# Choosing experts and building their gate rows side by side in one stage: broadcast one-hots, the factor on ScalarE, staging by 32 tokens

## The chip, the cores and the metric

One core of one Trainium2 chip runs the whole program. The metric is the device time of one execution in microseconds (us). TensorE, VectorE, ScalarE, GpSimd and SyncE each work off their own queue in order. In the profile's rows they are PE (with PEld for its weight loads), DVE, ACT, POOL and SP.

## The reference

Two transformer blocks over 512 tokens of width 1024, in fp32. The part that matters is the expert layer (`peer`) at the end of the first block:

```python
def chunk_fn(hc):
    q = (hc @ w_query).reshape(PEER_CHUNK, PEER_HEADS, PEER_KEY_DIM)
    s1 = jnp.einsum('chk,nk->chn', q[..., :PEER_HALF_DIM], keys_1)
    s2 = jnp.einsum('chk,nk->chn', q[..., PEER_HALF_DIM:], keys_2)
    v1, i1 = lax.top_k(s1, PEER_TOPK_HALF)
    v2, i2 = lax.top_k(s2, PEER_TOPK_HALF)
    cand = (v1[..., :, None] + v2[..., None, :]).reshape(PEER_CHUNK, PEER_HEADS, -1)
    cand_idx = (i1[..., :, None] * N_KEYS + i2[..., None, :]).reshape(PEER_CHUNK, PEER_HEADS, -1)
    top_s, pos = lax.top_k(cand, PEER_TOPK)
    experts = jnp.take_along_axis(cand_idx, pos, axis=-1)
    gate = jax.nn.softmax(top_s.astype(jnp.float32), axis=-1).astype(hc.dtype)
    u = jnp.take(expert_u, experts, axis=0)
    act = jax.nn.gelu(jnp.einsum('chkd,cd->chk', u, hc))
    v = jnp.take(expert_v, experts, axis=0)
    return jnp.einsum('chk,chkd->cd', gate * act, v)
```

There are 8 heads, 16 chosen experts per head (128 per token) and 16384 experts, addressed by two indices of 128 values each.

## The kernel before

Three of the four token tiles (384 tokens) are computed densely: the activations of all 16384 experts, in 128 groups of 128 experts, are made by TensorE, multiplied by a gate matrix that is zero where an expert was not chosen, and multiplied with the V matrix. The fourth tile gathers its own experts' rows by indirect DMA (`pick`) and reduces them on VectorE.

Work goes by an order written out by hand (`manual_schedule`): each engine takes its instructions in program order. The unit of that order is a *slot*, made by `slot()`. Slot i issues the load of expert group i+3 (`u_load`, SP queue), prepares group i+2 (`u_prep`: ScalarE makes `uhi`, VectorE makes `ulo`), runs what is passed as `dve`, then multiplies group i (`u_main`: 24 matrix products into `act`, below called a U block), runs what is passed as `after`, applies the gelu (`ga`, ScalarE), writes it to DRAM (`asc`, issued by ScalarE), issues some of the waiting gate pieces (`piece`, SP) and some gathered rows (`pick`, a GpSimd gather and one VectorE operation on `row`). There are three `uhi` and three `ulo` buffers and two `act` buffers in PSUM.

Before the change two loops of slots follow each other:

- **Choosing.** For each of the four token tiles, the generator `choose(t)` is stepped once per slot. A tile has seven steps of VectorE work: candidates and the first and second half of the top 16 (steps 1, 2), the `ge` comparison and its products (3), reductions and products that read the two indices out (4 to 6), softmax (7, with an `Exp` on ScalarE). The seventh step falls into the slot of the next tile's first, so there are 24 slots, and one more (`CGAP`).
- **Gates.** The gate matrix of 8 tokens is a *unit*, and there are 48. `gate_rows` makes for each token a one-hot row `ob` over the second index and a one-hot row `oa` over the first, times the gate, each [128 chosen, 128]. `gate_mm` multiplies them one slot later on TensorE (8 products into `pg`), and ScalarE copies `pg` into the staging tile `st`. When 64 tokens are staged, 8 pieces of 512 KB are queued for DRAM (`gsc`), one issued per slot. Units are made at 7 in 8 slots. `gate_t` transposes the indices and gates of a tile ahead of its first unit.

After the last unit, slots without gate work issue the last pieces two at a time, and a few more bring the slot number to an even start. Then a list of jobs mixes the rest of the U groups with the V products: `v_load` reads the V rows (`vraw`), the spilled activations (`va`) and, for every second group, the gates (`vg`); `v_prep` multiplies activation and gate; `v_main` runs 18 products into `pv`.

Of the kernel before, what the change touches and what calls it, by code (L numbers as in the profile page):

```python
# [7 lines left out]
F32 = mybir.dt.float32  # L8
# [4 lines left out]
AF = mybir.ActivationFunctionType  # L13
ALU = mybir.AluOpType
# [6 lines left out]
P = 128  # L21
# [4 lines left out]
TD = 384  # L26
NH = 8
NE = 128
TB = 8
OB = 2  # L30
NTAP = 7
WINDOWS = (8, 15, 16, 17)
UPS = (7, 8)
TG = 64
IB = 16
CPICK, CGAP = (0, 1, 0, 0, 1, 0, 0), (1,)
BPICK, BDRAIN = 1, 2
BRIDGE = 2
MASK = -1.0e30
# [20 lines left out]
def body(nc, tc, A, out, stop=None):  # L60
# [23 lines left out]
    iotaf = const.tile([P, P], F32, name="iotaf")  # L84
# [13 lines left out]
    def split(hi, lo, src, lo_eng=None):  # L98

        nc.scalar.copy(hi, src)  # L100
        (lo_eng or nc.vector).tensor_sub(lo, src, hi.bitcast(F32))  # L101
# [176 lines left out]
    start = tc.manual_schedule()  # L278
# [17 lines left out]
    ps = lin.bank()  # L296
# [13 lines left out]
    first = [lin.bank() for _ in range(8)]  # L310
    H = []
    for k in range(DC):
# [9 lines left out]
        hi, lo = whl.pop(k)  # L322
# [299 lines left out]
    Asc = {}  # L622
    Gsc = [dram.tile([TD // TG, P, IB * TG], F32, name=f"gsc{b}") for b in range(NE // IB)]

    gb = {"ulo": nc.vector}


    U = {}
# [6 lines left out]
    def u_prep(i):  # L635
        hi = upool.tile([P, DC, P], F32R, tag="uhi", name="uhi", bufs=3)
        lo = upool.tile([P, DC, P], F32R, tag="ulo", name="ulo", bufs=3)
        split(hi, lo, U[i][0], gb["ulo"])
        U[i] = [hi, lo]

    def u_main(i):
# [51 lines left out]
        nc.scalar.copy(gb["t3"], pt)  # L693

    def gate_rows(t, q):
        if q == 0:
            gate_t(t)
        t3 = gb["t3"]
        ob = gp.tile([P, TB, P], F32, tag="ob", name="ob", bufs=OB)
        oa = gp.tile([P, TB, P], F32, tag="oa", name="oa", bufs=OB)  # L700
        for j in range(TB):
            of = lambda n: t3[:, n, q * TB + j:q * TB + j + 1]
            nc.vector.tensor_scalar(ob[:, j], iotaf, of(1), None, op0=ALU.is_equal)
            nc.vector.tensor_scalar(oa[:, j], iotaf, of(0), of(2), op0=ALU.is_equal, op1=ALU.mult)
        return t, q, ob, oa

    def gate_mm(t, q, ob, oa):

        g, o = divmod(t * P + q * TB, TG)
        if o == 0:  # L710
            gb["st"] = gp.tile([P, P, TG], F32, tag="st", name="st", bufs=2)
        for h in range(TB // 4):
            ps = pg.tile([P, 4, P], F32, tag="pg", name="pg", bufs=5)
            for j in range(4):
                nc.tensor.matmul(ps[:, j], ob[:, 4 * h + j], oa[:, 4 * h + j], start=True, stop=True)  # L715
            nc.scalar.copy(gb["st"][:, :, o + 4 * h:o + 4 * h + 4].rearrange("p i t -> p t i"), ps)
        if o + TB == TG:
            for b in range(NE // IB):
                pieces.append((Gsc[b][g], gb["st"][:, b * IB:(b + 1) * IB].rearrange("p i t -> p (i t)")))
# [14 lines left out]
    def slot(dve=None, after=None, picks=0, drain=1):  # L734
        nonlocal ui
        i = ui
        ui += 1
        if i + 3 < NE:
            u_load(i + 3)
        u_prep(i + 2)  # L740
        r = dve() if dve else None
        u_main(i)
        if after:
            after()
        u_post(i, True)
        piece(drain)
        pick(picks)
        return r

    for n, t in enumerate([GT] + list(range(GT))):  # L750
        for n2, _ in enumerate(choose(t)):
            slot(picks=CPICK[n2] if n > 1 or n == 1 and n2 > 1 else 0)
    for n in CGAP:
        slot(picks=n)
    tk.close()
    vvs.close()
    gs = ExitStack()
    gp = R(gs, "gp")
    pg = pool(gs, "pg", 1, space=PSUM)
    units = [(t, q) for t in range(GT) for q in range(P // TB)]  # L760
    ready = []
    nu = 0
    first = ui
    while nu < len(units) or ready:
        mine = []
        want = (ui - first + 1) * UPS[0] // UPS[1]
        old, ready = ready, []

        def dve():
            nonlocal nu  # L770
            while nu < min(want, len(units)):
                ready.append(gate_rows(*units[nu]))
                nu += 1

        def after():
            for o in old:
                gate_mm(*o)
        slot(dve, after, 1)
    while pieces:
        slot(picks=BPICK, drain=BDRAIN)  # L780
    gs.close()


    vs = ExitStack()
# [7 lines left out]
    def v_load(i):  # L792
        raw = vp.tile([P, D], F32, tag="vraw", name="vraw", bufs=4)
        nc.sync.dma_start(raw, A["v"][i * P:(i + 1) * P, :])
        a = None
        kind = "s" if i in Asc else "d"
        if i % 2 == 0:
            VG[kind] = vp.tile([P, TD // TG, 2, TG], F32, tag=f"vg{kind}", name="vg", bufs=2 + (kind == "s"))
            o = i % IB * TG
            nc.sync.dma_start(VG[kind].rearrange("p g i t -> p g (i t)"),  # L800
                              Gsc[i // IB][:, :, o:o + 2 * TG].rearrange("g p n -> p g n"))
        g = VG[kind][:, :, i % 2]
        if i in Asc:
            a = vp.tile([P, TD], F32, tag="va", name="va", bufs=4)
            nc.sync.dma_start(a, Asc[i])
        V[i] = raw, g, a
# [23 lines left out]
                    hi[:, s2 * S:(s2 + 1) * S], lo[:, s2 * S:(s2 + 1) * S], nv == 0, nv == NE - 1)  # L830
        nv += 1

    if (ui + BRIDGE) % 2:
        slot(picks=BPICK)
    direct = list(range(ui + BRIDGE, NE))
    spilled = list(range(ui + BRIDGE))
# [420 lines left out]
```

## Time and profile before

| | |
|---|---|
| Median of 3 runs | 2670.35 us (2669.46 to 2670.9) |
| The profiled execution's own time | 2670.35 us |
| Its span | 2668.6 us |
| First product of the U groups starts | 438.4 us |
| First and last start of the gate products | 590.0 and 896.8 us |
| First V product starts | 938.3 us |

The span is the part of the execution that the trace covers. A row of a group of instructions gives how many there were, their time in sum and the mean of one. Matmul ends are modelled, so what a product costs TensorE is read from the distance between starts. Each fp32 gate product appears as two instructions.

### The profile page before, as it was taken

What the parts mean: (1) busy time and instruction counts of PE and PEld (TensorE: products, weight loads), DVE (VectorE), ACT (ScalarE), POOL (GpSimd) and SP (SyncE); (2) the same over time, 40 slices, a digit from 0 to 9 for tenths busy, and PEclk for the clock granted to TensorE, in tenths of its full rate; (3) what the DMA queues carried; (4) which work ended last, traced back from release to release, by engine and by line L of the source; (5) the groups of instructions that cost most, each with busy time, mean ns of one, the idle gap of its engine ahead of it and who ended that gap; (6) DMA issues with size and microseconds to landing.
All of it is one profiled execution on the core that took longest, in us unless ns stands there. A gap on an engine that the chain in (4) does not pass through costs nothing.

```text
span 2668.6 us, 33504 instructions
## 1 busy us (share of the span) xinstructions
PE 2562.1 (96%) x12307; PEld 2151.7 (81%) x12307; DVE 1852.4 (69%) x3791; ACT 983.4 (37%) x1374; POOL 456.7 (17%) x323
## 2 busy tenths in 40 slices
PE   6988999889999999999999998999999999999998
PEld 4766778889999988888888886778888675788886
DVE  6999578999999777778787788544334575544423
ACT  3324332345555433333333335222222554422221
POOL 0000231012222233333434341000010000100000
PEclk9998999999999999999999999999999999999999
DMA  8435320567878899999999992322333221222232
GB/s 297 152 119 165 128 76 29 173 193 259 299 275 322 318 361 332 338 336 334 334 340 328 349 338 88 103 91 93 94 97 108 84 79 44 87 95 95 95 91 75
DMA packets 205061, 508.05 MB, mean 190 GB/s; under 512 B 18208, under 2 KB 94496, under 8 KB 204896
## 3 DMA queue, kind: packets, MB, share of 16 engines
q1 hardware_dynamic: 154928, 354.18, 39.6%
q0 software_dynamic: 36864, 134.23, 13.9%
q10 hardware_dynamic: 13104, 17.50, 1.8%
q8 instruction: 97, 1.59, 0.2%
q14 instruction: 68, 0.56, 0.1%
HBM read 461.23 MB, written 44.61 MB: 190 GB/s over the span
## 4 chain that ended last, share of the span: by engine, by line
PE 83%; DVE 11%; DMA 3%; issue 2%; ACT 1%; SPq 0%; ACTq 0%; DVEq 0%
PE mm L105 14%; PE mm L104 14%; PE mm L106 14%; PE pv L105 6%; PE pv L106 6%; PE pv L104 6%; PE act L106 5%; PE act L104 5%; PE act L105 5%; PE pg L715 3%; DVE ycv L336 2%; PE s L1070 1%; DVE ulo L101 1%; DVE wlo L101 1%; PE o L1095 1%
## 5 line engine op out<-in xcount | busy, mean ns | idle before, releaser
L101 DVE TENSOR_TENSOR wlo<-raw,whi 128x1024 fp32r<-128x1024 f32 x212 | 257.7, 1217 | 337.9 <-ACT whi L100 333.2
L100 ACT CAST whi<-raw 128x1024 fp32r<-128x1024 f32 x228 | 235.2, 1034 | 657.4 <-PE mm L105 545.7
L106 PE MATMUL act<-h2h,ulo 128*128 128x384 f32 x1024 | 347.7, 340 | 22.9 <-DVE ulo L101 22.7
L104 PE MATMUL act<-h2h,uhi 128*128 128x384 f32 x1024 | 349.3, 341 | 2.1 <-ACT ga L650 2.1
L105 PE MATMUL mm<-gl,whi 128*128 128x512 f32 x864 | 344.8, 399 | 2.5 <-DVE gl L208 2.4
L105 PE MATMUL act<-h2l,uhi 128*128 128x384 f32 x1024 | 345.0, 337 | 0.0
L106 PE MATMUL mm<-gh,wlo 128*128 128x512 f32 x864 | 342.8, 397 | 1.5 <-DVE wlo L101 1.5
L104 PE MATMUL mm<-gh,whi 128*128 128x512 f32 x864 | 342.7, 397 | 0.4 <-DVE x L885 0.4
L104 PE MATMUL pv<-vhi,ch 128*128 128x512 f32 x768 | 299.3, 390 | 1.6 <-ACT ch L819 1.6
L105 PE MATMUL pv<-vlo,ch 128*128 128x512 f32 x768 | 300.3, 391 | 0.0
L106 PE MATMUL pv<-vhi,cl 128*128 128x512 f32 x768 | 300.3, 391 | 0.0
L680 POOL DMA_INDIRECT row<-in_u_dram,idx x128 | 183.7, 1435 | 538.6 <-DVE act L663 475.5
L820 DVE TENSOR_TENSOR vlo<-vraw,vhi 128x1024 fp32r<-128x1024 f32 x128 | 156.4, 1222 | 135.9 <-ACT vhi L814 135.9
L680 POOL DMA_INDIRECT row<-in_v_dram,idx x128 | 183.1, 1430 | 268.9 <-DVE gacc L671 246.4
L106 PEld LDWEIGHTS act<-h2h,ulo 128*128 128x128 f32 x1024 | 194.0, 189 | 29.3 <-DVE ulo L101 29.0
L179 POOL TENSOR_TENSOR sq<-sq 128x512 f32<-128x512 f32 x24 | 37.6, 1569 | 959.1 <-ACT sq L173 958.5
L814 ACT CAST vhi<-vraw 128x1024 fp32r<-128x1024 f32 x128 | 134.4, 1050 | 174.4 <-issue 161.0
L105 PEld LDWEIGHTS mm<-gl,whi 128*128 128x128 f32 x864 | 162.5, 188 | 44.2 <-DVE gl L208 3.8
L104 PEld LDWEIGHTS act<-h2h,uhi 128*128 128x128 f32 x1024 | 194.3, 190 | 4.3 <-ACT ga L650 2.8
L104 PEld LDWEIGHTS mm<-gh,whi 128*128 128x128 f32 x864 | 162.4, 188 | 42.6 <-issue 2.3
L106 PEld LDWEIGHTS mm<-gh,wlo 128*128 128x128 f32 x864 | 162.5, 188 | 41.3 <-issue 2.0
L105 PEld LDWEIGHTS act<-h2l,uhi 128*128 128x128 f32 x1024 | 194.3, 190 | 1.5
(824 smaller groups left out, 4915.3 us busy)
## 6 DMA issues: line engine op xcount, KB each, us to landing
uraw<-in_uT_dram SPq DMA_DIRECT2D x128, 512.0 KB, 5.9
vraw<-in_v_dram SPq DMA_DIRECT2D x128, 512.0 KB, 5.8
raw<-in_w_in_dram SPq DMA_DIRECT2D x52, 512.0 KB, 3.6
gsc<-st SPq DMA_DIRECT2D x48, 512.0 KB, 9.1
vg<-gsc SPq DMA_DIRECT2D x64, 384.0 KB, 6.7
raw<-in_ffn_w_gate_dram SPq DMA_DIRECT2D x44, 512.0 KB, 3.6
raw<-in_ffn_w_up_dram SPq DMA_DIRECT2D x44, 512.0 KB, 3.4
raw<-in_ffn_w_down_dram SPq DMA_DIRECT2D x40, 512.0 KB, 3.6
```

Source lines behind the costliest of these rows:

```text
L100: nc.scalar.copy(hi, src)
L101: (lo_eng or nc.vector).tensor_sub(lo, src, hi.bitcast(F32))
L104: nc.tensor.matmul(ps, whi, ahi, start=first, stop=False)
L105: nc.tensor.matmul(ps, whi, alo, start=False, stop=False)
L106: nc.tensor.matmul(ps, wlo, ahi, start=False, stop=last)
L179: self.eng.tensor_add(self.acc, self.acc, t)
L336: nc.vector.scalar_tensor_tensor(ycv[c], glu[c][:, j:j + S], dw(c, j), ycv[c], op0=ALU.mult, op1=ALU.add)
L680: nc.gpsimd.indirect_dma_start(out=r, out_offset=None, in_=A[table], in_offset=bass.IndirectOffsetOnAxis(ap=idx[:, k:k + 1], axis=0))
L715: nc.tensor.matmul(ps[:, j], ob[:, 4 * h + j], oa[:, 4 * h + j], start=True, stop=True)
L814: nc.scalar.copy(hi, raw)
L820: nc.vector.tensor_sub(lo, raw, hi.bitcast(F32))
L1070: nc.tensor.matmul(ps[:, :n], qt[r0:r0 + 64, i * P:(i + 1) * P], kt[r0:r0 + 64, :n], start=True, stop=True)
```

## The change

- One loop of slots replaces the two. The generator steps go at two in three slots for the first 21 slots (the gathered tile and the first dense tile), then at one in three; from slot 22 on, units go at two in three slots, and from slot 62 on at one per slot. A unit of tile t waits until the tile is chosen.
- `ob` and `oa` of a unit are made by one VectorE operation each over [128, 8 x 128], with both inputs broadcast. The multiplication of `oa` by the gate moves to ScalarE, 8 operations of 128 columns with a scale per partition, one slot later (`gate_times`). The products come another slot later. There are three buffers of `ob` and `oa` where there were two.
- The product of a token goes to every fourth column of `pg` ([128, 128, 4]), and the copy into `st` writes runs of 4 tokens.
- Staging is by 32 tokens: 96 pieces of 256 KB in place of 48 of 512 KB, two issued per slot. A `vg` load covers four groups (768 KB) in place of two (384 KB).
- The slots before the job list end at a multiple of four: 92 groups are spilled where there were 88, and 36 stay direct where there were 40. Gathered rows start in slot 11.

The place in which `ulo` is made (`gb["ulo"]`) stays VectorE. The diff, without the two hunks that only say that:

```diff
@@ -27,13 +27,12 @@
 NH = 8
 NE = 128
 TB = 8
-OB = 2
+OB = 3
 NTAP = 7
 WINDOWS = (8, 15, 16, 17)
-UPS = (7, 8)
-TG = 64
+TG = 32
+GI = 4
 IB = 16
-CPICK, CGAP = (0, 1, 0, 0, 1, 0, 0), (1,)
 BPICK, BDRAIN = 1, 2
 BRIDGE = 2
 MASK = -1.0e30
...
@@ -693,15 +692,24 @@
         nc.scalar.copy(gb["t3"], pt)
 
     def gate_rows(t, q):
+
         if q == 0:
             gate_t(t)
         t3 = gb["t3"]
         ob = gp.tile([P, TB, P], F32, tag="ob", name="ob", bufs=OB)
         oa = gp.tile([P, TB, P], F32, tag="oa", name="oa", bufs=OB)
+        k0 = q * TB
+        shape = [P, TB, P]
+        row = lambda n: t3[:, n, k0:k0 + TB, None].to_broadcast(shape)
+        cols = iotaf[:, None, :].to_broadcast(shape)
+        nc.vector.tensor_tensor(ob, cols, row(1), op=ALU.is_equal)
+        nc.vector.tensor_tensor(oa, cols, row(0), op=ALU.is_equal)
+        return t, q, ob, oa, t3
+
+    def gate_times(t, q, ob, oa, t3):
         for j in range(TB):
-            of = lambda n: t3[:, n, q * TB + j:q * TB + j + 1]
-            nc.vector.tensor_scalar(ob[:, j], iotaf, of(1), None, op0=ALU.is_equal)
-            nc.vector.tensor_scalar(oa[:, j], iotaf, of(0), of(2), op0=ALU.is_equal, op1=ALU.mult)
+            k = q * TB + j
+            nc.scalar.activation(oa[:, j], oa[:, j], AF.Copy, scale=t3[:, 2, k:k + 1])
         return t, q, ob, oa
 
     def gate_mm(t, q, ob, oa):
@@ -710,10 +718,10 @@
         if o == 0:
             gb["st"] = gp.tile([P, P, TG], F32, tag="st", name="st", bufs=2)
         for h in range(TB // 4):
-            ps = pg.tile([P, 4, P], F32, tag="pg", name="pg", bufs=5)
+            ps = pg.tile([P, P, 4], F32, tag="pg", name="pg", bufs=5)
             for j in range(4):
-                nc.tensor.matmul(ps[:, j], ob[:, 4 * h + j], oa[:, 4 * h + j], start=True, stop=True)
-            nc.scalar.copy(gb["st"][:, :, o + 4 * h:o + 4 * h + 4].rearrange("p i t -> p t i"), ps)
+                nc.tensor.matmul(ps[:, :, j], ob[:, 4 * h + j], oa[:, 4 * h + j], start=True, stop=True)
+            nc.scalar.copy(gb["st"][:, :, o + 4 * h:o + 4 * h + 4], ps)
         if o + TB == TG:
             for b in range(NE // IB):
                 pieces.append((Gsc[b][g], gb["st"][:, b * IB:(b + 1) * IB].rearrange("p i t -> p (i t)")))
@@ -747,38 +755,41 @@
         pick(picks)
         return r
 
-    for n, t in enumerate([GT] + list(range(GT))):
-        for n2, _ in enumerate(choose(t)):
-            slot(picks=CPICK[n2] if n > 1 or n == 1 and n2 > 1 else 0)
-    for n in CGAP:
-        slot(picks=n)
-    tk.close()
-    vvs.close()
+
+
     gs = ExitStack()
     gp = R(gs, "gp")
     pg = pool(gs, "pg", 1, space=PSUM)
     units = [(t, q) for t in range(GT) for q in range(P // TB)]
-    ready = []
-    nu = 0
-    first = ui
-    while nu < len(units) or ready:
-        mine = []
-        want = (ui - first + 1) * UPS[0] // UPS[1]
+    gens = [choose(t) for t in torder]
+    made, ready = [], []
+    steps = nu = n = 0
+    while nu < len(units) or made or ready:
+        csteps = 2 * (n + 1) // 3 if n < 21 else min(28, 14 + (n - 20) // 3)
+        want = max(0, (n - 20) * 2 // 3) if n < 62 else 28 + (n - 62)
         old, ready = ready, []
+        eqs, made = made, []
 
         def dve():
-            nonlocal nu
-            while nu < min(want, len(units)):
-                ready.append(gate_rows(*units[nu]))
+            nonlocal nu, steps
+            while steps < csteps:
+                next(gens[steps // 7], None)
+                steps += 1
+            while nu < min(want, len(units), max(0, steps // 7 - 1) * (P // TB)):
+                made.append(gate_rows(*units[nu]))
                 nu += 1
+            ready.extend(gate_times(*e) for e in eqs)
 
         def after():
             for o in old:
                 gate_mm(*o)
-        slot(dve, after, 1)
+        slot(dve, after, 1 if n > 20 or n > 10 and n % 3 == 2 else 0, 2)
+        n += 1
     while pieces:
         slot(picks=BPICK, drain=BDRAIN)
     gs.close()
+    tk.close()
+    vvs.close()
 
 
     vs = ExitStack()
@@ -794,12 +805,14 @@
         nc.sync.dma_start(raw, A["v"][i * P:(i + 1) * P, :])
         a = None
         kind = "s" if i in Asc else "d"
-        if i % 2 == 0:
-            VG[kind] = vp.tile([P, TD // TG, 2, TG], F32, tag=f"vg{kind}", name="vg", bufs=2 + (kind == "s"))
-            o = i % IB * TG
-            nc.sync.dma_start(VG[kind].rearrange("p g i t -> p g (i t)"),
-                              Gsc[i // IB][:, :, o:o + 2 * TG].rearrange("g p n -> p g n"))
-        g = VG[kind][:, :, i % 2]
+        if (kind, i // GI) not in VG:
+            for k in [k for k in VG if k[0] == kind]:
+                del VG[k]
+            vg = VG[kind, i // GI] = vp.tile([P, TD // TG, GI, TG], F32, tag=f"vg{kind}", name="vg", bufs=2)
+            o = i // GI * GI % IB * TG
+            nc.sync.dma_start(vg.rearrange("p g i t -> p g (i t)"),
+                              Gsc[i // IB][:, :, o:o + GI * TG].rearrange("g p n -> p g n"))
+        g = VG[kind, i // GI][:, :, i % GI]
         if i in Asc:
             a = vp.tile([P, TD], F32, tag="va", name="va", bufs=4)
             nc.sync.dma_start(a, Asc[i])
@@ -830,7 +843,7 @@
                     hi[:, s2 * S:(s2 + 1) * S], lo[:, s2 * S:(s2 + 1) * S], nv == 0, nv == NE - 1)
         nv += 1
 
-    if (ui + BRIDGE) % 2:
+    while (ui + BRIDGE) % GI:
         slot(picks=BPICK)
     direct = list(range(ui + BRIDGE, NE))
     spilled = list(range(ui + BRIDGE))
```

Where it moves instructions, VectorE's queue at the start of the stage before the change (`II` is the last of the query's top 16, `cand` to `pos` the first step of choosing, `ulo` belongs to the third U group):

```order
L532 MAX_INDEX II<-VV,rep 128x8 x4
L570 CAST IF<-II 128x256
L575 TENSOR_TENSOR cand<-VV 128x8x16
L575 TENSOR_TENSOR cand<-VV 128x8x8
L575 TENSOR_TENSOR cand<-VV 128x8x5
L575 TENSOR_TENSOR cand<-VV 128x8x4
L575 TENSOR_TENSOR cand<-VV 128x8x3
L575 TENSOR_TENSOR cand<-VV 128x8x6
L575 TENSOR_TENSOR cand<-VV 128x8x8
L524 MAX ts<-cand 128x8 x4
L526 MAX_INDEX pos<-ts,cand 128x8 x4
L528 MATCH_REPLACE rep<-ts,cand 128x50 x4
```

Behind these come two more rows of the step and only then the third `ulo`. In the changed kernel the same place reads as follows; the third `ulo` stands far ahead, beside the first two, and the one shown is the fourth:

```order
L529 MAX VV<-rep 128x8 x4
L531 MAX_INDEX II<-VV,rep 128x8 x4
L100 TENSOR_TENSOR ulo<-uraw,uhi 128x1024
L569 CAST IF<-II 128x256
L574 TENSOR_TENSOR cand<-VV 128x8x16
L574 TENSOR_TENSOR cand<-VV 128x8x8
```

So two `ulo` moved ahead of the first step of choosing.

VectorE's queue in the changed kernel, some slots after the first unit, where choosing (tile 1, second step: `ts` to `pf`) and units stand beside each other (`row` and `act` are the gathered tile's reduction):

```order
L705 TENSOR_TENSOR ob<-iotaf,t_4328 128x1024
L706 TENSOR_TENSOR oa<-iotaf,t_4328 128x1024
L662 ISA row,act<-row,h2t 128x1024
L662 ISA act 128x1
L100 TENSOR_TENSOR ulo<-uraw,uhi 128x1024
L523 MAX ts<-cand 128x8 x4
L525 MAX_INDEX pos<-ts,cand 128x8 x4
L527 MATCH_REPLACE rep<-ts,cand 128x50 x4
L529 MAX ts<-rep 128x8 x4
L531 MAX_INDEX pos<-ts,rep 128x8 x4
L584 TENSOR_TENSOR ex<-ts 128x128
L586 CAST pf<-pos 128x128
```

Two operations of 1024 columns stand where 16 of 128 stood, and a step of choosing stands between units, where before all steps stood ahead of all units.

ScalarE's queue for one slot with a unit, before:

```order
L100 CAST uhi<-uraw 128x1024
L716 COPY st<-pg 128x4x128 x2
L650 ACTIVATE ga<-act 128x384
L654 DMA asc_4780<-ga 128x384
L100 CAST uhi<-uraw 128x1024
```

and in the changed kernel:

```order
L99 CAST uhi<-uraw 128x1024
L712 ACTIVATE oa<-oa,t_4328 128x128 x8
L724 COPY st<-pg 128x128x4 x2
L649 ACTIVATE ga<-act 128x384
L653 DMA asc_4506<-ga 128x384
```

The eight operations with the factor stand between the conversion and the copies of an earlier unit's products.

## Rows read from the trace of the kernel before

**Rows 1.** The page: span, and busy time by engine.

```profile
span 2668.6 us, 33504 instructions
PE 2562.1 (96%) x12307; PEld 2151.7 (81%) x12307; DVE 1852.4 (69%) x3791; ACT 983.4 (37%) x1374; POOL 456.7 (17%) x323
```

**Rows 2.** Windows: stretch, length, busy by engine (instructions), TensorE clock, DMA share, GB/s.

```profile
492.00:524.00 32.00, 28.27 (x156) 26.57 (x155) 31.41 (x104) 12.90 (x17) 0.00 (x0) 1.00 0.43 142
640.00:690.00 50.00, 50.00 (x337) 50.00 (x337) 47.83 (x148) 27.47 (x34) 14.07 (x9) 1.00 0.88 307
1020.00:1220.00 200.00, 200.00 (x951) 174.20 (x950) 156.99 (x218) 70.38 (x98) 73.05 (x57) 1.00 0.96 337
```

**Rows 3.** Tile views of act, pg, pv: ns min/median/max of one, first and last start.

```profile
L104 PE MATMUL act<-h2h,uhi x1024: 331/334/525, 438.4 to 1591.8; 128*128 128x384 f32 x171
...
L715 PE MATMUL pg<-oa,ob x768: 272/275/275, 590.0 to 896.8; 128*128 128x128 f32 x192
...
L104 PE MATMUL pv<-vhi,ch x21: 387/389/628, 938.3 to 959.9; 128*128 128x512 f32 x21
```

**Rows 4.** The chain that ended last: start us, us, what.

```profile
242.24 3.56 PE mm L159 x8
...
459.77 2.21 DVE ge L591
...
491.62 2.21 DVE ge L591
...
625.85 1.78 PE pg L715 x16
635.96 1.78 PE pg L715 x16
```

**Rows 5.** Waits from 440 to 590: who, for whom; us in sum, times, longest.

```profile
PE act L106 <- DVE ulo L101: 22.2, 11, 6.1
```

**Rows 6.** Timeline of VectorE, start of choosing: start us, us, instruction.

```profile
449.77 0.27 DVE L570 CAST IF<-II 128x256 bf16<-128x256 uint32 x1
...
454.04 1.21 DVE L101 TENSOR_TENSOR ulo<-uraw,uhi 128x1024 fp32r<-128x1024 f32 x1
...
459.68 2.29 DVE L591 TENSOR_TENSOR ge<-pf,starts 128x2048 bf16<-128x2048 bf16 x1
...
464.83 1.22 DVE L101 TENSOR_TENSOR ulo<-uraw,uhi 128x1024 fp32r<-128x1024 f32 x1
```

**Rows 7.** Timeline of VectorE, one unit among the gates.

```profile
642.41 1.22 DVE L101 TENSOR_TENSOR ulo<-uraw,uhi 128x1024 fp32r<-128x1024 f32 x1
643.55 0.28 DVE L703 TENSOR_SCALAR ob<-iotaf,t 128x128 f32<-128x128 f32 x1
...
647.17 1.22 DVE L663 CUSTOM_DVE_ANT_0 row<-row,h2t 128x1024 f32<-128x1024 f32 x1
```

**Rows 8.** Groups of ScalarE, whole span: shapes, count, busy us, mean ns, idle before.

```profile
L716 ACT COPY st<-pg 128x512 f32<-128x512 f32 x96 | 96.6, 1100 | 104.0 <-PE pg L715 104.0
L100 ACT CAST uhi<-uraw 128x1024 fp32r<-128x1024 f32 x128 | 134.2, 1050 | 60.4 <-DMA uraw<-in_uT_dram 28.1 <-DVE oa L704 20.2 <-ACT ga L650 5.7
L650 ACT ACTIVATE ga<-act 128x384 f32<-128x384 f32 x128 | 65.0, 508 | 260.3 <-PE act L106 260.3
L543 ACT COPY scs<-sp 128x512 f32<-128x512 f32 x16 | 9.4, 588 | 6.0 <-ACT scs L543 4.0 <-PE sp L540 1.3 <-DVE VV L524 0.7
```

**Rows 9.** Timelines of ScalarE: operations with a column of numbers (x7 merged), and one.

```profile
1632.22 4.39 ACT L925 ACTIVATE sq<-x,vec 128x512 f32<-128x512 f32 x7
...
2103.91 0.40 ACT L1076 ACTIVATE s__17675<-s__17675,st__17676 128x128 f32<-128x128 f32 x1
```

**Rows 10.** Windows of TensorE behind the gates: stretch, length, busy (instructions), clock, DMA, GB/s.

```profile
915.00:920.00 5.00, 3.92 (x21) 1.00 1.03 418
...
945.00:950.00 5.00, 3.42 (x12) 0.88 1.08 374
950.00:955.00 5.00, 5.00 (x19) 0.78 1.02 392
```

More of the change, by code (lines that the diff above doesn't have):

```diff
@@ L623, in body @@
     Gsc = [dram.tile([TD // TG, P, IB * TG], F32, name=f"gsc{b}") for b in range(NE // IB)]
-    gb = {"ulo": nc.vector}
+    gb = {}
     U = {}
@@ L637, in u_prep @@
         lo = upool.tile([P, DC, P], F32R, tag="ulo", name="ulo", bufs=3)
-        split(hi, lo, U[i][0], gb["ulo"])
+        split(hi, lo, U[i][0])
         U[i] = [hi, lo]
```

## The prediction

> **What bounds the kernel now.** I read the page first: TensorE is busy for 2562.1 of 2668.6 us [rows 1], so only time in which it waits, or in which it could work on something shorter, is to be had. Then the windows show where it waits [rows 2]: among the gates (640 to 690) it is busy throughout, and so it is later among the V products (1020 to 1220); in the choosing stage (492 to 524) it is busy 28.27 of 32 us while VectorE is busy 31.41.
>
> How much that costs follows from the price of a U block. Between the two gate groups at 625.85 and 635.96 lie 1.78 us of gate products and two U blocks [rows 4], so a block is (10.11 - 1.78) / 2 = 4.165 us. From the first U product at 438.4 to the first gate product at 590.0 [rows 3] are 151.6 us. By the code 28 blocks lie in it: 25 slots of choosing, then a slot without a unit, one that makes the first, one whose block precedes its products. 28 blocks are 116.6 us; some 2.4 us are score products and transposes (an estimate at the 0.11 us of a gate instruction, 1.78 / 16). So 32.6 us are lost. The waits name the cause: TensorE waited for `ulo`, 11 times, 22.2 us, the longest 6.1 [rows 5]; the rest passed at a lower clock behind such waits or at weight loads.
>
> From the first gate product to the last nothing is lost: VectorE's unit takes 647.17 - 643.55 = 3.62 us for 16 operations [rows 7], plus `ulo` (1.14) and `row` (about 1.2), 5.96 in all, and TensorE 4.165 + 1.78 = 5.94. The stage runs at both engines' limit, so units alone could not go faster.
>
> Behind the gates lies a second loss. Nine U blocks (81 slots have passed, 90 blocks precede the first V product) are 37.5 us; from the end of the last gate products (896.8 plus about a microsecond) to 938.3 [rows 3] pass some 40.4. The windows show fewer products at a DMA share of 1.02 to 1.08 [rows 10]: 21 between 915 and 920 where 5 / 4.165 x 24 = 28.8 fit; later 12 and 19 in 5 us, at a granted clock of 0.88 and 0.78 of 2.4 GHz, where the V stage has 951 / 40 = 23.8 [rows 2]. The latter is (23.8 - 12 + 23.8 - 19) / 23.8 x 5 = 3.5 us. Together about 6.4. So 39 us can be won.
>
> **The start of the stage.** The third `ulo` waited behind the first step of choosing, which takes 454.04 - 449.77 = 4.3 us [rows 6]. It now stands with the first two, and the fourth ahead of that step: the wait of 6.1 us goes. The fourth would end at about 451, and block 3 starts at 438.4 + 2.4 + 3 x 4.165 = 453.3. I count nothing for what is left.
>
> **VectorE's load.** A tile takes 491.62 - 459.77 = 31.85 us [rows 4] with six `ulo`; without them 25.0, so 3.6 us a step on average and 464.83 - 459.68 = 5.2 at the longest [rows 6]. Six blocks are 25.0 us: at one step per slot VectorE is always late by 6.9 us per tile. In the changed kernel the first 21 slots hold 14 steps (50.4), 21 `ulo` (23.9) and 4 `row` (4.8), 79 us against 87.5 of TensorE: hidden.
>
> A unit is now two operations of 1024 columns with broadcast inputs. `ulo` has their size and type, 1.14 us each to the next start [rows 7]; `ge`, whose inputs are broadcast in the same way, takes 2.29 for 2048 columns [rows 6], the same per column. So 2.28 us instead of 3.62. The upper bound is that nothing is won, 3.62. Slots 21 to 62 hold 14 steps (50.4), 28 units (63.8), 42 `ulo` and 42 `row` (98.3): 212.5 us, against 42 x 4.165 + 28 x 1.78 = 224.8 of TensorE. It fits with 5% to spare. Of three slots, 15.2 of 16.05 us; but a group with the longest step takes 16.8, and VectorE can't use every gap, since each `ulo` waits for a `uhi` that ScalarE makes behind the copies and gelu of the block before. For 14 such groups I allow 0.6 us each, 8 us. From slot 63 on, 20 units, 22 `ulo` and 22 `row` are 97 us against 127: hidden.
>
> **ScalarE's load.** Per slot `uhi` 1.05 and `ga` 0.51 [rows 8]. A factor on 128 columns: with a column of factors 512 take 4.39 / 7 = 0.63 us in a row [rows 9]; 384 columns fewer at (1.05 - 0.51) / 640 = 0.85 ns leave 0.30. At most it is 0.40, the whole duration of the 128-column operation in [rows 9]. Eight are 2.4 us (at most 3.2). The two copies cost 1.10 each now, writing single words 64 apart; a contiguous copy of that size costs 0.59 [rows 8]. Runs of four lie between, and I take 0.59 as nearer to a contiguous write. A slot with a unit then costs 1.56 + 2.4 + 1.2 = 5.2 us, against 5.94 of TensorE: hidden; at both upper ends 1.56 + 3.2 + 2.2 = 7.0, which is not. The factors wait a turn, so they ask for a unit that VectorE made a slot earlier, and the copies stand behind them.
>
> On the price of the copy the Trainium skill (SBUF — State Buffer, Specifications) speaks for the low end: a 16-byte line needs two or more hits for full bandwidth. The copy of now hits each line once, the new one four times; by that rule the sum stands as I make it, and with 1.10 it would be the second rival below.
>
> **TensorE's own work** stays: as many products, blocks and transposes. What is new is that a product's columns go 16 bytes apart into PSUM. No row shows that. From below it costs nothing: fp32 products of 512 columns take 3.56 / 8 = 0.445 us an instruction [rows 4], 0.87 ns per column, as the gate products do (0.111 us for 128); a U product takes 4.165 / 24 = 0.174 us for 384, 0.45 ns per column. PSUM so takes columns at twice the rate at which gate products bring them, and a write up to 1.9 times slower stays hidden. From above, writes four times slower make an instruction 0.22 us: 768 x 0.111 = 85 us. I take nothing, and keep both ends.
>
> The Trainium skill (PSUM — Partial Sum Buffer, Specifications) speaks against the change here: lines are 8 bytes, and any non-contiguous pattern slows matmuls significantly. It gives no figure; taken as doubling these instructions it is the first rival, and if it means half the contiguous rate, it costs nothing here.
>
> **Behind the gates.** After the last unit 8 pieces of 256 KB are left, not 512: 2.1 MB less at 418 GB/s [rows 10], 5 us of DMA; the first two `vg` loads are 384 KB larger each, 2 us back. Of the 6.4 us I keep 3. Four more spilled groups move 4 x 192 KB out and in again; no block is added. The V stage runs at a DMA share of 0.96 with TensorE always busy [rows 2]; larger `vg` loads are issued four jobs ahead, some 16 us, and hidden; if they were not, each of 32 could cost a microsecond.
>
> **The sum.** The execution takes 2670.35 us (span 2668.6 and 1.75 around it), which is also the median of the runs. Less 39, plus 8 (groups of three slots), plus 2 (products at a lower clock behind such waits, an allowance), plus 3 (behind the gates): 2644 us.
>
> **Rivals.** (1) Strided PSUM writes: gate products at 0.22 us an instruction, which decides as soon as writes are more than 1.9 times slower than contiguous. TensorE gets 85 us more, and VectorE's 8 vanish behind it: 2644 + 85 - 8 = 2721, slower. For it speaks that no row shows such a write, against it the slack of 1.9. (2) ScalarE becomes late: 7.0 us per slot loses 1.06 in each of 20 slots, and in the groups of three its 3 x 1.56 + 2 x 5.4 = 15.5 of 16.05 us leave no room behind VectorE, say 0.5 us more in 14: 2644 + 21 + 7 = 2672, no change; at half of that, 2658. (3) The broadcast operations save nothing: 28 x 1.34 = 37.5 us more in slots 21 to 62, less the 12.3 to spare: 2669. `ge` speaks against it. (4) The time is handed on: the V stage can't take its transfers faster, or late `vg` loads cost up to 32 us: 2655 to 2676. Its TensorE is never idle, against it. (5) VectorE's queue has no jitter and the allowances fall: 2631.
>
> **How the numbers follow.** The forecast with its allowances halved or nearly doubled, 2634 to 2656: 0.62. Below it: 0.06. ScalarE late (2): 0.12, half of it within 0.2% (5.3 us, about what a measurement of this kernel can tell from no change). (3) and (4) together: 0.08, a third within, a sixth slower. (1): 0.12. So faster 0.78, same 0.09, slower 0.13. The range leaves out (1) and the lowest end: 2631 to 2680.
>
> **What the trace would show.** Right: waits of TensorE for `ulo` before 590 of under 3 us, the first gate product at about 546, first V product near 934 with 94 blocks ahead of it; `ob` and `oa` 1.2 us each; factors 0.40 long and 0.30 apart; copies of `pg` near 0.6; gate instructions 0.11 us apart. Wrong: gate instructions 0.2 us apart (1); copies still 1.1 and TensorE waiting for factors (2); TensorE waiting for `ulo` or `oa` in every third slot by more than a microsecond; DMA waits ahead of `va` or `ga` products after 1000.

## The result, and the profile after

The changed kernel takes 2641.85 us (median of 4 runs, 2640.63 to 2643.65) against 2670.62 for the kernel before (4 runs, 2669.46 to 2672.7): a ratio of 0.9892, 95% interval 0.9875 to 0.9909. The profiled execution took 2642.09 us, 28.3 less than that of before.

The page, with the rows that answer to [rows 1]:

```profile
span 2640.3 us, 33245 instructions
...
PE 2553.7 (97%) x12307; PEld 2147.4 (81%) x12307; DVE 1792.2 (68%) x3119; ACT 1055.2 (40%) x1758; POOL 426.1 (16%) x323
```

TensorE has as many instructions as before. VectorE has 672 fewer and 60 us less to do, ScalarE 384 more and 72 us more.

The tile views of `act`, `pg` and `pv` (ns min/median/max of one, first and last start), which answer to [rows 3]:

```profile
L103 PE MATMUL act<-h2h,uhi x1024: 332/334/444, 439.5 to 1564.0; 128*128 128x384 f32 x171
...
L723 PE MATMUL pg<-oa,ob x768: 271/275/377, 545.7 to 891.8; 128*128 128x128 f32 x192
...
L103 PE MATMUL pv<-vhi,ch x768: 387/389/494, 929.3 to 1596.5; 128*128 128x512 f32 x192
```

By the prices of the prediction (a U block 4.165 us, a unit's products 1.78) these starts give the account of the stage, which here begins 1.1 us later than before. From the first U product to the first gate product are 106.2 us, and 25 blocks with their scores and transposes are 104.1 + 2.4: nothing is lost, where 32.6 us were. From the first to the last gate product are 346.1 us; 60 blocks (249.9), 48 units (85.4) and transposes (1.3) are 336.6, so 9.5 us are lost, where none were. From there to the first V product are 37.5 us, which are nine blocks: nothing is lost. Counted in the same way, 41.5 - 37.5 = 4.0 were lost before; the prediction, which gave the end of the gates a microsecond, had 2.9.

The windows (stretch, length, busy by engine with instructions, granted clock, DMA share, GB/s) answer to [rows 2]:

```profile
492.00:524.00 32.00, 32.00 (x186) 32.00 (x185) 29.00 (x94) 11.88 (x15) 0.15 (x1) 1.00 0.66 230
640.00:690.00 50.00, 49.56 (x319) 49.18 (x318) 43.28 (x118) 36.76 (x83) 13.07 (x9) 1.00 0.88 313
700.00:730.00 30.00, 28.50 (x176) 27.80 (x175) 26.11 (x33) 21.21 (x51) 8.58 (x6) 1.00 0.79 278
800.00:895.00 95.00, 95.00 (x640) 95.00 (x639) 69.46 (x77) 76.41 (x182) 14.99 (x16) 1.00 0.84 298
...
1020.00:1220.00 200.00, 200.00 (x948) 173.85 (x947) 156.65 (x210) 70.27 (x98) 75.05 (x55) 1.00 0.94 334
```

At 492 to 524 TensorE is busy throughout, with 186 products for 156. At 700 to 730 lies part of what is lost among the gates, at a granted clock of 1.00. In the V stage nothing has changed. The start of the V products, where [rows 10] showed 31 products in 10 us:

```profile
930.00:940.00 10.00, 8.92 (x37) 6.64 (x36) 5.46 (x9) 4.25 (x7) 1.89 (x2) 1.00 1.07 373
940.00:950.00 10.00, 10.00 (x51) 8.92 (x51) 7.46 (x12) 2.93 (x5) 3.70 (x3) 1.00 1.07 377
```

At the 23.8 products in 5 us of [rows 2] 95 would fit; 88 are there, 1.5 us lost where 3.5 were. The DMA share is as high as before, but the clock stays at its full 2.4 GHz. All told 9.5 + 1.5 = 11.0 us are lost, where 32.6 + 4.0 + 3.5 = 40.1 were: 29.1 are won, less the 1.1 of the later start, which is the 28.3 of the spans within a few tenths. (The stage begins between 437.0 and 441.5 us in the profiled runs of this document, with the same program ahead of it, so 1.1 us there says nothing about the change.)

The groups of ScalarE and of VectorE (count, busy us, mean ns of one, idle before), which answer to [rows 7, 8]:

```profile
L712 ACT ACTIVATE oa<-oa,t 128x128 f32<-128x128 f32 x384 | 117.6, 389 | 47.4 <-DVE oa L706 47.4
L724 ACT COPY st<-pg 128x512 f32<-128x512 f32 x96 | 52.7, 580 | 12.2 <-PE pg L723 12.2
```

```profile
L706 DVE TENSOR_TENSOR oa<-iotaf,t 128x1024 f32<-128x1024 f32 x48 | 58.5, 1220 | 0.0
L705 DVE TENSOR_TENSOR ob<-iotaf,t 128x1024 f32<-128x1024 f32 x48 | 58.5, 1219 | 0.0
```

`ob` and `oa` cost what `ulo` costs, the copy in runs of 4 words 0.58 us, as a contiguous one did. The factor lasts 0.39, and eight in a row 2.45 (in the chain below seven take 2.15), so their starts are 0.30 apart. New is that ScalarE waits 47.4 us, in 23 waits, for `oa` of VectorE.

The chain of waits, over one slot with a step of choosing and the next one (start us, us, what):

```profile
595.62 1.09 DVE x L599
...
596.76 1.23 DVE ob L705
597.99 1.14 DVE oa L706
...
599.15 0.06 ACT oa L712
...
599.46 2.15 ACT oa L712 x7
601.61 0.95 ACT st L724 x2
602.56 0.39 ACT ga L649
...
603.34 1.06 ACT uhi L99
...
604.43 0.07 DVE ulo L100
...
605.57 1.22 DVE ob L705
```

TensorE is not in this stretch of it. VectorE makes a unit only after the step (`x` is its last operation); ScalarE stands at the factor of that unit; copies, gelu and `uhi` stand behind the factors, and VectorE's next `ulo` waits for that `uhi`. TensorE, which has two `act` buffers, waits for the gelu. Its waits from 430 to 960, all there are, in us, times and longest:

```profile
PE act L103 <- ACT ga L649: 4.1, 7, 0.8
PE pv L103 <- ACT ch L832: 1.0, 1, 1.0
PE pg L723 <- ACT oa L712: 0.6, 1, 0.6
```

No wait for `ulo` is left ([rows 5]: 22.2 us). Of the 9.5 us lost among the gates these rows show 4.7. The waits of TensorE's weight loads for the same two, from 546 to 895, come to 7.7:

```profile
PEld act L103 <- ACT ga L649: 6.3, 10, 1.0
PEld pg L723 <- ACT oa L712: 1.4, 3, 0.9
```

The timeline of TensorE shows a part that no wait counts: the products of one unit without a late factor, then those of one whose factors come late, and the first product of the U block behind it.

```profile
600.93 1.95 PE L723 MATMUL pg<-oa,ob 128*128 128x128 f32 x16
...
617.50 2.53 PE L723 MATMUL pg<-oa,ob 128*128 128x128 f32 x16
620.88 0.44 PE L103 MATMUL act<-h2h,uhi 128*128 128x384 f32 x1 [0.85 <-ACT ga L649]
```

ScalarE starts on the late factors at 617.04. The products follow them one factor at a time, and the unit takes 2.53 us instead of 1.95.

### The profile page after: what moved, and what is told of

It reads as the page before. It is cut to its first block, busy times and chain, and to the rows that moved or that the text cites. A ratio compares the mean times of both kernels' runs of the same rounds, so it can differ in the third digit from the quotient of the medians.

```text
span 2640.3 us, 33245 instructions
## 1 busy us (share of the span) xinstructions
PE 2553.7 (97%) x12307; PEld 2147.4 (81%) x12307; DVE 1792.2 (68%) x3119; ACT 1055.2 (40%) x1758; POOL 426.1 (16%) x323
## 4 chain that ended last, share of the span: by engine, by line
PE 82%; DVE 10%; DMA 3%; ACT 3%; issue 2%; SPq 0%; ACTq 0%; DVEq 0%
PE mm L103 14%; PE mm L104 14%; PE mm L105 14%; PE pv L104 7%; PE pv L105 7%; PE pv L103 7%; PE act L103 5%; PE act L105 5%; PE act L104 5%; DVE ycv L335 2%; PE pg L723 2%; PE s L1083 1%; DVE wlo L100 1%; ACT oa L712 1%; PE o L1108 1%
## 5 line engine op out<-in xcount | busy, mean ns | idle before, releaser
L679 POOL DMA_INDIRECT row<-in_u_dram,idx x128 | 159.8, 1248 | 526.3 <-DVE act L662 456.7
L679 POOL DMA_INDIRECT row<-in_v_dram,idx x128 | 176.4, 1378 | 283.0 <-DVE gacc L670 255.7
L100 DVE TENSOR_TENSOR ulo<-uraw,uhi 128x1024 fp32r<-128x1024 f32 x128 | 156.2, 1222 | 73.2 <-ACT uhi L99 73.0
```

Of the source, the lines that this page charges most:

```text
L679: nc.gpsimd.indirect_dma_start(out=r, out_offset=None, in_=A[table], in_offset=bass.IndirectOffsetOnAxis(ap=idx[:, k:k + 1], axis=0))
```

## The experiments

Each experiment is an edit of the changed kernel (2641.85 us). Ratios are against the kernel before, from runs on the same chip, 95% intervals. The kernel before took 2669.04 to 2669.82 us in these sets of runs and 2670.62 in that of the changed kernel, so a microsecond or two between the medians of two edits says nothing.

**Which part of the change earns the time.** The order of the two loops of before, all else as changed:

```diff
-        csteps = 2 * (n + 1) // 3 if n < 21 else min(28, 14 + (n - 20) // 3)
-        want = max(0, (n - 20) * 2 // 3) if n < 62 else 28 + (n - 62)
+        csteps = min(28, (n + 1) * 7 // 6)
+        want = max(0, n - 24) * 7 // 8
```

> The changed kernel with its two activities one after the other again: all 28 steps of choosing in the first 24 slots, then units at 7 in 8 slots; broadcast one-hots, factors on ScalarE, strided products and staging by 32 stay. Theory (the gain is that choosing no longer takes a slot per step): four tiles lose 6.9 us each again, 27.6, and the 9.6 us of waits in the groups of three slots go; with some 3 us at the start, where the first step stands ahead of the fourth ulo again: 2660 to 2666 us. Rival (the cheaper units, copies and pieces by themselves give the gain): 2640 to 2645 us.

Measured: 2664.92 us, 0.9985 (0.9975 to 0.9994). The waits of TensorE from 438 to 600, and the tile view of `pg`:

```profile
PE act L105 <- DVE ulo L100: 19.8, 14, 3.0
```

```profile
L723 PE MATMUL pg<-oa,ob x768: 271/275/275, 591.6 to 898.8; 128*128 128x128 f32 x192
```

Choosing waits as before, and the gates take 307.2 us, as before (306.8): units that are cheaper for VectorE are worth nothing there, because TensorE is full. The first V product starts at 932.2, 33.4 us behind the last gate product, which are eight blocks: so the loss behind the gates goes without the mixed order too, and most of the gain of some 5 us is that. Which of the other parts does it, the staging, the loads or the shorter copies, was not separated. In the mixed order the staging and the loads don't assure it: two edits further down keep both, and nine blocks behind their gates take 41.8 us (old one-hots) and 42.0 (single words) where 37.5 are needed. The other 23 us need the mixed order.

**What the mixed order needs.** Three edits take one part of the units back. The old one-hots, without the factor on ScalarE (the loop over `j` with two `tensor_scalar` in `gate_rows`, as in the diff's minus lines, and `gate_times` empty):

```diff
-        nc.vector.tensor_tensor(ob, cols, row(1), op=ALU.is_equal)
-        nc.vector.tensor_tensor(oa, cols, row(0), op=ALU.is_equal)
+        for j in range(TB):
+            of = lambda n: t3[:, n, q * TB + j:q * TB + j + 1]
+            nc.vector.tensor_scalar(ob[:, j], iotaf, of(1), None, op0=ALU.is_equal)
+            nc.vector.tensor_scalar(oa[:, j], iotaf, of(0), of(2), op0=ALU.is_equal, op1=ALU.mult)
```

> The changed kernel with the old one-hot rows: 16 VectorE operations of 128 columns per unit, the factor in them, none on ScalarE; the order of slots stays. Theory (VectorE has 12 us to spare in slots 21 to 62 and the cheaper unit pays for the steps of choosing there): 28 units cost 1.34 us more, 37.5, less 12.3 to spare, and ScalarE's waits go: 2657 to 2667 us, with TensorE waiting for ulo or oa in every group of three slots. Rival (the order alone gives the gain, VectorE has room enough): 2640 to 2645 us.

Measured: 2655.35 us, 0.9948 (0.9931 to 0.9964), 13.5 slower than the changed kernel. TensorE waits for `ulo` again, 438 to 940:

```profile
PE act L105 <- DVE ulo L100: 10.1, 11, 1.4
```

The time is just below the range of the theory. So what the new units save on VectorE matters here. The edit takes back the broadcast and the move of the factor together; the next one takes back the factor alone. The gates take 354.8 us, 8.7 more than in the changed kernel, and 4.3 are lost behind them.

The factor on VectorE as a third broadcast operation, `gate_times` empty:

```diff
         nc.vector.tensor_tensor(oa, cols, row(0), op=ALU.is_equal)
+        nc.vector.tensor_tensor(oa, oa, row(2), op=ALU.mult)
```

> The changed kernel with the factor as a third VectorE operation of 1024 columns per unit in place of eight on ScalarE. Theory (VectorE has little room in slots 21 to 62): 28 x 1.14 = 32 us more less 12.3 to spare is 20, less 5 to 9 us of waits for the factors on ScalarE: 2650 to 2660 us. Rival (VectorE has room, the wait for ScalarE is what is left): below 2640 us.

Measured: 2648.11 us, 0.9922 (0.9906 to 0.9939), 6.3 slower: below the range of the theory and above that of the rival. The tile view of `pg` and TensorE's wait:

```profile
L721 PE MATMUL pg<-oa,ob x768: 271/275/531, 543.3 to 895.8; 128*128 128x128 f32 x192
```

```profile
PE pg L721 <- DVE oa L707: 10.5, 7, 2.6
```

The gates take 352.5 us, 16 lost. The load that the prediction counted would be 28 x 1.14 = 32 us more than 212.5, so 20 over the 224.8 of TensorE.

The products of a token side by side in `pg`, and single words written by the copy, as before:

```diff
-                nc.tensor.matmul(ps[:, :, j], ob[:, 4 * h + j], oa[:, 4 * h + j], start=True, stop=True)
-            nc.scalar.copy(gb["st"][:, :, o + 4 * h:o + 4 * h + 4], ps)
+                nc.tensor.matmul(ps[:, j], ob[:, 4 * h + j], oa[:, 4 * h + j], start=True, stop=True)
+            nc.scalar.copy(gb["st"][:, :, o + 4 * h:o + 4 * h + 4].rearrange("p i t -> p t i"), ps)
```

> The changed kernel with the products of a token side by side in pg, as before, and the copy into st writing single words 32 apart. Theory (ScalarE is near its limit): a copy costs 1.1 us again, 1.0 more per unit; at one unit per slot ScalarE takes 6.2 of 5.94 us, some 6 us over 20 slots, and in the groups of three the factors come later, 5 to 10 us: 2650 to 2660 us. Rival (ScalarE has slack): 2640 to 2645 us. Both: gate instructions stay 0.111 us apart, as with the strided write.

Measured: 2658.74 us, 0.9961 (0.9947 to 0.9975), 16.9 slower. The copy's tile view, and TensorE's waits from 438 to 940:

```profile
L724 ACT COPY st<-pg x96: 1034/1110/1206, 548.0 to 906.3; 128x512 f32<-128x512 f32 x96
```

```profile
PE act L103 <- ACT ga L649: 16.3, 13, 2.7
PE pg L723 <- ACT oa L712: 1.1, 2, 0.6
```

The copy is slow again, and now ScalarE is late: this is the mechanism of the second rival, made by hand. It has only the copy at its upper bound, not the factor, and lies at the lower of the rival's two figures (2658). The gates take 360.2 us, 14.1 more than in the changed kernel; 4.5 are lost behind them. In [rows 8] the same copy cost nothing, since ScalarE had time.

**The steps at two in three slots.** One step per slot until tile 0 is chosen:

```diff
-        csteps = 2 * (n + 1) // 3 if n < 21 else min(28, 14 + (n - 20) // 3)
+        csteps = min(14, n + 1) if n < 21 else min(28, 14 + (n - 20) // 3)
```

> The changed kernel with one step of choosing in each of the first 14 slots and none in slots 14 to 20, in place of two in three slots; all else, the early third ulo too, stays. Theory (a slot's U block can't cover a step and a ulo on VectorE): two tiles lose 6.9 us each again, less what the third ulo gives as a lead, so 8 to 14 us: 2650 to 2656 us, with TensorE waiting for ulo before the first gate product. Rival (what the start won is the place of the third ulo alone): 2640 to 2645 us.

Measured: 2652.74 us, 0.9932 (0.9915 to 0.9948), 10.9 slower; first gate product at 555.2 instead of 545.7. TensorE's wait before it:

```profile
PE act L105 <- DVE ulo L100: 6.7, 4, 2.0
```

VectorE, once late, does not give the time back: TensorE has then already waited. The prediction had VectorE late by 6.9 us per tile at this pace, 13.8 for the two. The third `ulo`'s place alone doesn't make the gain.

**Where the 9.5 us among the gates go.** My theory from the chain: the unit stands behind the step in VectorE's queue, and the factor ahead of copies and gelu in ScalarE's, so a late `oa` stops ScalarE for both. The rival was the prediction's own reason: VectorE has too much to do in a group of three slots. Three edits change an order and leave each engine's work as it is. The step in each group of three slots falls one slot later, into the slot that makes no unit:

```diff
-        csteps = 2 * (n + 1) // 3 if n < 21 else min(28, 14 + (n - 20) // 3)
+        csteps = 2 * (n + 1) // 3 if n < 21 else min(28, 14 + (n - 21) // 3)
```

> The changed kernel with the steps of choosing one slot later from slot 21 on, so that a step falls into the slot of each three that makes no unit. Theory (the 9 to 10 us lost between the first and last gate product come from a unit that stands behind a step on VectorE: its factors, and behind them copies, gelu and the next conversion on ScalarE, wait): those waits of ScalarE for oa, 47 us in sum, fall to under 20 and TensorE wins 5 to 9 us: 2633 to 2638 us. Rival (VectorE is simply full in slots 21 to 62, 212 of 225 us): no change, 2640 to 2643 us.

Measured: 2634.24 us, 0.9866 (0.9849 to 0.9882), gates 547.1 to 884.9 (337.8 us), with a single wait of TensorE there, 1.1 us for the gelu. ScalarE's wait for `oa` (47.4 in the changed kernel):

```profile
ACT oa L712 <- DVE oa L706: 11.8, 15, 3.0
```

The unit is made ahead of the step (in `dve()`, the loop over units stands first):

```diff
-            while steps < csteps:
-                next(gens[steps // 7], None)
-                steps += 1
             while nu < min(want, len(units), max(0, steps // 7 - 1) * (P // TB)):
                 made.append(gate_rows(*units[nu]))
                 nu += 1
+            while steps < csteps:
+                next(gens[steps // 7], None)
+                steps += 1
```

> The changed kernel with the unit ahead of the step of choosing in VectorE's order within a slot. Theory as for the shifted step: the factors no longer wait for a step, and 5 to 9 us are won: 2633 to 2638 us. The rival (VectorE full): no change, 2640 to 2643 us.

Measured: 2631.7 us, 0.9858 (0.9842 to 0.9875), a little below the expected range. The tile view of `pg`, ScalarE's wait for `oa`, and VectorE's timeline over the same slots as above:

```profile
L723 PE MATMUL pg<-oa,ob x768: 271/275/275, 543.7 to 880.0; 128*128 128x128 f32 x192
```

```profile
ACT oa L712 <- DVE oa L706: 0.6, 2, 0.3
```

```profile
602.34 1.23 DVE L100 TENSOR_TENSOR ulo<-uraw,uhi 128x1024 fp32r<-128x1024 f32 x1 [0.75 <-ACT uhi L99]
603.49 1.22 DVE L705 TENSOR_TENSOR ob<-iotaf,t 128x1024 f32<-128x1024 f32 x1
604.62 1.22 DVE L706 TENSOR_TENSOR oa<-iotaf,t 128x1024 f32<-128x1024 f32 x1
605.76 1.64 DVE L562 TENSOR_TENSOR x<-x 128x1024 bf16<-128x1024 bf16 x3
...
608.17 2.29 DVE L604 TENSOR_TENSOR x<-sa,iotab 128x2048 bf16<-128x2048 bf16 x1
```

`ob` and `oa` come ahead of the step (`x`, `sa`). The gates take 336.3 us, the 336.6 that the blocks and units need: nothing is lost, with VectorE's work unchanged. ScalarE's wait for `oa` is down from 47.4 us to 0.6. So VectorE's load by itself doesn't cost the 9.5 us.

The starts of TensorE's products in the two traces say where the changed kernel loses them. Its gates take 9.8 us more than these (346.1 against 336.3). Summed over the stage, 6.8 of that lie before the first product of a U block behind a unit (the gelu is late), 0.9 before the first product of a unit and 1.8 between the products of a unit (the factors are late), and 0.3 inside U blocks.

The factors behind the gelu in ScalarE's queue, VectorE's order as changed:

```diff
-            ready.extend(gate_times(*e) for e in eqs)
...
         slot(dve, after, 1 if n > 20 or n > 10 and n % 3 == 2 else 0, 2)
+        ready.extend(gate_times(*e) for e in eqs)
```

> The changed kernel with the factors behind the copies and the gelu of their slot on ScalarE, not ahead of them. Theory (what TensorE waits for is the gelu, which frees an act buffer and stands behind factors that wait for VectorE): its waits for ga, 4.1 us, go to none, and most of the 9 to 10 us with them: 2633 to 2639 us. Rival (the wait for the factors only moves to the next conversion, uhi, which stands behind them then): 2640 to 2645 us.

Measured: 2634.93 us, 0.9872 (0.9856 to 0.9889), gates 543.6 to 879.8:

```profile
L723 PE MATMUL pg<-oa,ob x768: 271/275/275, 543.6 to 879.8; 128*128 128x128 f32 x192
```

ScalarE comes to the factors later and waits 3.5 us for `oa`, with copies and gelu already done; TensorE waits for neither. Either order removes the loss, so it took both to make it. With both edits together:

> The changed kernel with the unit ahead of the step on VectorE and the factors behind the gelu on ScalarE. Theory (each alone already takes away the wait for a unit behind a step, and from the first to the last gate product nothing was lost any more): as with the unit ahead of the step, 2629 to 2634 us. Rival (each mends another part): 2622 to 2627 us.

Measured: 2633.07 us, 0.9859 (0.9843 to 0.9876), gates 544.3 to 880.6: as one edit alone.

**What a product's strided write costs.** In the chain of the changed kernel a unit's products take what they took in [rows 4], 16 instructions in 1.78 us:

```profile
764.89 1.78 PE pg L723 x16
```

To see a limit behind that, the gate products were fed faster: `ob` and `oa` in bf16 (8 instructions a unit in place of 16), once with `pg` as changed, once with `pg` and copies as in the edit above.

```diff
-        ob = gp.tile([P, TB, P], F32, tag="ob", name="ob", bufs=OB)
-        oa = gp.tile([P, TB, P], F32, tag="oa", name="oa", bufs=OB)
+        ob = gp.tile([P, TB, P], BF16, tag="ob", name="ob", bufs=OB)
+        oa = gp.tile([P, TB, P], BF16, tag="oa", name="oa", bufs=OB)
```

> A measurement: the changed kernel with the one-hot rows in bf16, so that gates are rounded to bf16 and a gate product is one instruction in place of two; it writes 16 bytes apart as the changed kernel does. Read are the distances between the starts of gate products. If a strided write takes one column in no more than 0.45 ns, they are as in the contiguous twin; if it takes one in 0.87 ns, at least 0.11 us.

> Its twin with the products of a token side by side in pg and the copy writing single words, the gates rounded to bf16 as well. The distance between gate products is that of a contiguous write: below 0.11 us, by the 0.45 ns a column of U products some 0.06 to 0.08 us.

Measured, one run each: 2632.43 and 2660.87 us. A unit's products in TensorE's timeline, eight merged, and the tile view for one; first strided:

```profile
L723 PE MATMUL pg<-oa,ob x384: 269/314/373, 547.8 to 877.3; 128*128 128x128 bf16 x192
```

```profile
804.22 1.05 PE L723 MATMUL pg<-oa,ob 128*128 128x128 bf16 x8
```

and contiguous:

```profile
L723 PE MATMUL pg<-oa,ob x384: 215/219/232, 546.4 to 904.4; 128*128 128x128 bf16 x192
```

```profile
801.76 0.62 PE L723 MATMUL pg<-oa,ob 128*128 128x128 bf16 x8
```

Eight last from the first start to the last end, so the distance between starts is (1.05 - 0.314) / 7 = 0.105 us strided and (0.62 - 0.219) / 7 = 0.057 contiguous: a strided write costs 1.8 times as much, 0.82 ns per column instead of 0.45. An fp32 product brings a column every 0.87 ns, so it hides this just so. Both distances come from one run each. The edit that writes the U products themselves 16 bytes apart gave no result, so no run shows the strided write at their rate.

The second kernel is slow for ScalarE's sake (copies of 1.08 us again), not for its products, like the kernel with single words in the copies.

## Why the prediction was right, and where its reasons were not

- **The sum.** 2644 predicted, 2641.85 measured, in the range of 2631 to 2680 and on the forecast side. Of its terms: 39 to be won, of which 32.6 in choosing went whole; of the loss behind the gates 1.5 is left, where 3 were kept, and it was a microsecond larger than the prediction had it; 9.5 of 10 were lost among the gates. That is 1.5 + 1 + 0.5, 3 us better than the sum, and 1.1 worse for the later start, which differs from run to run.
- **Start of the stage.** Counted at nothing left; first gate product at 545.7 where "about 546" was said, first V product at 929.3 for "near 934": nothing was lost between the two stages.
- **VectorE's unit.** 2.28 us predicted; 1.14 and 1.14 from start to start (the chain's 1.23 is a whole duration). The third rival, which would give 2669, fell, and the experiment with the old one-hots shows that its bound was too high too: 2655.
- **ScalarE.** Factors 0.39 long and 0.30 apart and copies of 0.58, as predicted. With the copy at its upper bound the kernel is at 2659 (the experiment with single words), so this price decided 17 us. The Trainium skill (SBUF — State Buffer, Specifications) has a 16-byte line need two or more hits for full bandwidth: the trace agrees, 0.58 us for a copy in runs of four words against 1.11 in single ones.
- **TensorE's strided write.** Nothing was taken, and nothing was measured (1.78 us a unit). The slack of 1.9 by which the first rival was weighed turned out to be almost used up: the bf16 pair gives 1.8. The Trainium skill (PSUM — Partial Sum Buffer, Specifications) says that any non-contiguous pattern slows matmuls significantly: the bf16 pair agrees (0.105 us a product against 0.057); at the fp32 rate of this kernel the trace shows no difference, and there the measurement decides.
- **The step that failed, by reason and not by size.** The prediction allowed 8 us for groups of three slots, because a group with the longest step exceeds what TensorE covers, and 2 for the clock. 9.5 were lost, but the experiment with the unit ahead of the step has the same work on VectorE and loses nothing, and the granted clock was 1.00 in the windows at 640, 700 and 800. So the allowance came out near the measured loss by luck. The false sentence is the one under ScalarE's load: the factors "ask for a unit that VectorE made a slot earlier". That is so in the order of the program and not in time: behind a slot with a step they asked for a unit that VectorE had not made yet, 47.4 us of waiting, and everything behind them in ScalarE's queue waited along. The prediction did have the other half of the chain, that each `ulo` waits for a `uhi` which ScalarE makes behind the copies and gelu of the block before. The fifth rival (no jitter, 2631) gave the time that these orders reach: 2631.7, 2634.2 and 2634.9.
- **V stage.** 94 blocks ahead of it; no loss inside it, so the fourth rival fell: TensorE is busy throughout from 1020 to 1220.

What stays open is why the loss behind the gates is back in two of the experiments (41.8 and 42.0 us for nine blocks) though staging and loads are as changed. The interval of the best order (0.9842 to 0.9875) also meets that of the changed kernel at 0.9875, so the step from the one to the other rests on the medians, 10.2 us apart, on the runs themselves, which don't overlap (2629.9 to 2633.12 against 2640.63 to 2643.65), and above all on the spans of the gates, 336.3 against 346.1.

## What to carry to other kernels

When stages of different engines are mixed, count each engine's work, but then read the queues in order: an engine with time to spare still stops everything behind an operation whose input is late, and putting the urgent result ahead of the long step, or the waiting operation behind the urgent ones, can cost nothing, as here. A cost that lies beside other work is free only in that order of work: the slow copy cost nothing in the kernel before and 17 us in the mixed stage. And a price of "nothing" for a hidden cost should be given with its slack; here a factor of 1.9 hid 1.8.

## What the runs showed of the hardware

- A matrix product that writes fp32 columns 16 bytes apart into PSUM takes 0.105 us for 128 columns where a contiguous one takes 0.057 (bf16 inputs, one run each); at the fp32 rate of 0.111 us an instruction the stride doesn't show.
- A ScalarE operation on 128 columns with a factor per partition lasts 0.39 us, but eight in a row are 0.30 us apart, so 128 columns cost hardly less than half of 512 (0.63 in [rows 9]).
- Two VectorE inputs broadcast along different axes cost nothing extra at 1024 fp32 columns: 1.14 us from start to start, as the plain `ulo` [rows 7].
